# The SSD input tiles count as ready after 17 ticks in place of 12, and the SSD norm's row sums are issued one tick later

## The chip, the cores and the metric

The kernel runs on one core of a Trainium2 chip. The metric is the time of one execution on the device, in microseconds (us). Before the change the median of three runs is 1231.24 us (1230.96 to 1231.58).

A core has engines that run side by side, each through its own list of instructions in order: TensorE (PE: matmuls; its weight loads are shown as PEld), VectorE (DVE), ScalarE (ACT) and GpSimd (POOL); SyncE (SP) issues DMAs. They wait for one another through semaphores. PE writes to PSUM banks, and ACT or DVE must read a bank before PE may use it again.

## The reference, cut to what matters

One layer of a hybrid encoder on 256 tokens, model width 2048, in float32:

1. RMS norm, then one input projection whose columns serve two head groups. The SSD group (Mamba-2) takes x (1024 columns), B and C (256 each), z (1024) and dt (16); the GLA group takes q, k, v, a gate g and a low-rank gate.
2. SSD: x, B and C pass a causal convolution of width 4 over the tokens, then SiLU. With the decays from dt it computes, in chunks, `y = (C B^T, masked and decayed) (x dt) + state term + x d`, multiplies by SiLU(z), and takes an RMS norm over each half of 512 columns.
3. GLA: gated linear attention of 4 heads, its own norm and output gate.
4. Both results together pass the output projection and are added to x. Then a ConvFFN (up projection to 2 x 5632, a convolution of width 3, SiLU gate, down projection), a gate by an embedding of each token, and a final RMS norm.

## The kernel before

**Matmuls.** Everything is kept with channels on partitions and the 256 tokens as columns. Each float32 operand is split in a rounded part (hi) and a rest (lo). A product of one weight tile (128 x 128) with one activation tile is a *pair* of matmuls: L224 multiplies the weights' hi by both parts of the activation (512 columns), L226 the weights' lo by its hi (256 columns, 280 in a chunk's first one). ACT and DVE add the two halves of the bank (`combine`, L236 and L237).

**Weights.** They come from HBM in chunks of 1 MB (16 tiles), four buffers `raw`. `prepare` makes of each half chunk the hi part by a cast on ACT (L191) and the lo part by a subtraction on DVE (L192). There are five buffers of each, so a cast waits until PE has finished the half chunk five halves earlier.

**The input projection** goes through the list `PLAN`, one chunk at a time: v 0 to 3, conv 8 to 11 (B and C), conv 0, v 4, conv 1, v 5, conv 2, v 6, conv 3, v 7, conv 4, q 0, k 0, conv 5, v 8, conv 6, v 9, conv 7, v 10, q 1, k 1, v 11, q 2, k 2, q 3, k 3, then eight chunks z and eight g. A conv, q, k, z or g chunk is 16 pairs into one of four PSUM banks `pm_t`. Four v chunks share two banks, with 24 matmuls a chunk (L911 to L913, 352 columns). Behind each chunk its evacuation is written: for conv `ev_conv` (L561), with the combine, a multiplication by half the norm's factor (L563), the convolution (L565 on ACT, three L568 on DVE) and `half_silu` (a tanh on ACT, L444, then L445 on DVE). Conv 0 to 3 are the x tiles of the SSD's first half (group 0), conv 4 to 7 those of its second.

**Ticks.** All the attention work is written between these matmuls by small tasks (generators). `tick()` counts up after every 4 pairs (4 x 6 matmuls make the 4 ticks of a v chunk) and lets at most one task that is due take its next step. `mark(key, lag)` says that something counts as done `lag` ticks from now; `wait(keys)` holds a task until then. No instruction waits for a tick: they only decide in which place of PE's order, and so roughly when, a step stands. On PE that order is kept as written; the order on ACT and DVE is set by a scheduler that goes by its own estimates of times, so it changes with the places on PE.

**The SSD's tasks.** `ssd_rest` (L701) waits until the four x tiles of a group count as done. Then `ssd_xdt` (L637) transposes them on PE for the first 128 tokens (L640, four instructions into a bank `px_t`) and DVE multiplies by dt (L643) and, for the state, by a decay (L650); two ticks later the same for the other 128 tokens. Five ticks on, `ssd_state` makes the state by one matmul (L657) that ACT copies (L659), and `ssd_out` makes the outputs by 12 matmuls for each half of the group's tiles (L673, two pieces each in the trace), evacuated by DVE (L677). `ssd_front` makes the decays beside it (L615 loads on POOL's queue, L622, L630, L632, L633). After z, `ssd_norm` (L730) waits for the four tiles of a group and calls `norm_task` (L328): the sums over rows, a reciprocal root, two diagonal matrices (L317), and, `lag` ticks later, the matmuls that spread the factor over partitions (L325), its copy (L335) and the scaling and splitting of the four tiles (L737, L271, L272) that the output projection multiplies.

Of the kernel before, what the change touches and what calls it, by code (L numbers as in the profile page):

```python
# [99 lines left out]
def trunk(ctx, tc, wst, wv, xin, pin, prm_d, cst_d, gku_d, out):  # L100
# [14 lines left out]
    def slot(dtype=F32, shape=(128, 512)):  # L115
        return gpool.tile(list(shape), dtype, name="slot")

    def tmp():
        return small.tile([128, T], F32, name="tmp", bufs=10)
# [35 lines left out]
    def mark(key, lag=5):  # L155
        done[key] = now[0] + lag

    def wait(*keys):
        while any(done.get(k, 1 << 30) > now[0] for k in keys):
            yield 0  # L160
# [73 lines left out]
    def combine(ps):  # L234
        t = tmp()
        S.copy(out=t, in_=ps[:, T:2 * T])  # L236
        V.tensor_tensor(out=t, in0=ps[:, 0:T], in1=t, op=ALU.add)  # L237
        return t
# [20 lines left out]
    def pcol(i):  # L259
        return prm[:, i:i + 1]  # L260
# [8 lines left out]
    def split(src):  # L269
        a = slot(F32R, (128, 2, T))  # L270
        S.copy(out=a[:, 0, :], in_=src)  # L271
        V.tensor_tensor(out=a[:, 1, :], in0=src, in1=a[:, 0, :].bitcast(F32), op=ALU.subtract)  # L272
        return a
# [54 lines left out]
    def norm_task(sq, width, then, lag=6):  # L328
        with tc.high_priority(offset=2 * PRIO):
            r = sq.token(width)  # L330
            d = sq.spread(r)
        yield lag
        ps = sq.rows(d)
        keep = small.tile([128, T], F32, name="rb", bufs=2)
        S.copy(out=keep, in_=ps)  # L335
        then(r, keep)
# [105 lines left out]
    def half_silu(c, out):  # L442
        t = tmp()
        S.activation(out=t, in_=c, func=AF.Tanh)  # L444
        V.scalar_tensor_tensor(out=out, in0=t, scalar=1.0, in1=c, op0=ALU.add, op1=ALU.mult)  # L445
# [115 lines left out]
    def ev_conv(i, ps):  # L561
        v = combine(ps)
        V.tensor_tensor(out=v, in0=v, in1=state["rh"], op=ALU.mult)  # L563
        c = tmp()
        S.activation(out=c, in_=v, func=AF.Identity, scale=pcol(P_CW + 36 + i),  # L565
                     bias=cbh[:, i:i + 1])
        for s in (1, 2, 3):
            V.scalar_tensor_tensor(out=c[:, s:], in0=v[:, :T - s],  # L568
                                   scalar=pcol(P_CW + 12 * (3 - s) + i), in1=c[:, s:],
                                   op0=ALU.mult, op1=ALU.add)  # L570
        if i < 8:
            if i % 2 == 0:
                state["xs"] = slot()
            ssd_x[i] = state["xs"][:, (i % 2) * T:(i % 2 + 1) * T]
            half_silu(c, ssd_x[i])
        elif i < 10:
            half_silu(c, bT[:, (i - 8) * T:(i - 7) * T])
        else:
            half_silu(c, cT[:, (i - 10) * T:(i - 9) * T])
        mark(("conv", i), 12)  # L580

    cb = {}
    mt = {}
# [131 lines left out]
    ssd_sq = {}  # L715
# [14 lines left out]
    def ssd_norm():  # L730
        for g in range(2):
            yield from wait(("z", 4 * g + 3))

            def then(r, keep):
                for i in range(4 * g, 4 * g + 4):
                    y = ssd_y[i]
                    V.scalar_tensor_tensor(out=y, in0=y, scalar=pcol(P_SN + i), in1=keep,  # L737
                                           op0=ALU.mult, op1=ALU.mult)
                    mix[i] = split(y)
            yield from norm_task(ssd_sq[g], 512, then, 13)  # L740


    gq = [slot(), slot()]
# [121 lines left out]
    def ev_in(kind, i, ps):  # L865
        if kind == "conv":
            ev_conv(i, ps)
        elif kind == "q":
            ev_qk(gq, i, ps, 128.0 ** -0.5)
        elif kind == "k":  # L870
            ev_qk(gk, i, ps, 1.0)
            mark(("k", i))
        elif kind == "z":
            ev_z(i, ps)
        else:
            ev_g(i, ps)

    vps = None
    for ci, (kind, i) in enumerate(PLAN):
# [13 lines left out]
        if ci == 4:  # L893
            start(after(1, norm_task(sq_mix, 2048, in_norm, 6)))
            start(ssd_front())
            start(ssd_rest())
            start(gla_front())
            start(gla_back())
            start(ssd_norm())
# [64 lines left out]
    conv = {}  # L964
# [226 lines left out]
```

## Time and profile before

| what | value |
|---|---|
| median of three runs | 1231.24 us |
| profiled execution, its own time | 1230.86 us |
| its span, first to last instruction | 1228.9 us |
| mean granted clock of TensorE | 0.996 of full speed |
| PE busy | 1212.1 us, 99% |
| DVE busy | 916.8 us, 75% |
| ACT busy | 685.6 us, 56% |

The profile is of one execution. Its busy times say how full an engine is over the whole; which stage has the limit is seen in windows and in the timelines, where a row has its start, its length, engine, line and operation, the tile written and those read, and in square brackets the idle time of the engine before it with what ended it. Instructions of one engine overlap a little, so the next start tells better than the length how long one holds its engine. Times are counted from the start of the span.

### The profile page before, as it was taken

The page shows a single profiled execution, that of the slowest core. Times are in us where ns is not written, and L with a number is a line of the kernel's source. Part 1 is how long each engine was busy: PE and PEld are TensorE (multiplying, and loading weights), DVE is VectorE, ACT ScalarE, POOL GpSimd, SP SyncE. Part 2 cuts the span into 40 slices and gives each one's busy share as a digit, 9 for nine tenths or more (in the row PEclk, how much of TensorE's full clock was granted, in tenths as well). Part 3 has the DMA queues.
Part 4 walks back from the last instruction along what each step waited for, and adds up shares of the span by engine and source line. Part 5 has one row for each costly group of instructions (what it writes and reads, how often), then busy time and mean ns, then how long its engine had stood idle before and what let it go on. Part 6 is the DMA issues. An engine that isn't in the chain of part 4 may idle for free.

```text
span 1228.9 us, 18359 instructions
## 1 busy us (share of the span) xinstructions
PE 1212.1 (99%) x7115; PEld 1070.8 (87%) x7115; DVE 916.8 (75%) x1607; ACT 685.6 (56%) x1117; POOL 9.3 (1%) x23
## 2 busy tenths in 40 slices
PE   9998999999999999999999999999999999999996
PEld 8897888888888888888888888888888888888886
DVE  7889776789777788778875555878877876666775
ACT  8675555666544655555553333555555554444664
POOL 0010000000000000000000000000000000000000
PEclk9999999999999999999999999999999999999998
DMA  9855553444555555555555555555555555555632
GB/s 337 307 163 192 182 201 138 171 172 171 183 194 188 190 180 198 188 189 194 183 200 178 203 176 203 176 201 181 197 186 190 192 203 196 181 201 205 218 113 69
DMA packets 37623, 233.20 MB, mean 190 GB/s; under 512 B 4384, under 2 KB 4800, under 8 KB 11936
## 3 DMA queue, kind: packets, MB, share of 16 engines
q1 hardware_dynamic: 36832, 229.92, 53.2%
q0 software_dynamic: 704, 2.11, 0.6%
q8 instruction: 55, 0.90, 0.3%
q14 instruction: 32, 0.26, 0.1%
HBM read 227.81 MB, written 4.21 MB: 189 GB/s over the span
## 4 chain that ended last, share of the span: by engine, by line
PE 93%; DVE 3%; ACT 2%; issue 1%; DMA 1%; SPq 0%; DVEq 0%; ACTq 0%
PE pm_t L224 58%; PE pm_t L226 30%; DVE wlo L192 1%; PE pm_t L912 1%; PE pm_t L911 1%; PE pm_t L913 1%; ACT whi L191 1%; DMA raw<-in_wst_dram 1%; PE px_t L673 0%; ACT xg L264 0%; PE px_t L807 0%; DVE slot L630 0%; PE px_t L789 0%; ACT tmp L285 0%; PE px_t L292 0%
## 5 line engine op out<-in xcount | busy, mean ns | idle before, releaser
L224 PE MATMUL pm_t<-xg,whi 128*128 128x512 f32 x2224 | 778.7, 393 | 0.0
L191 ACT CAST whi<-raw 128x1024 fp32r<-128x1024 f32 (+3 forms) x444 | 445.2, 1007 | 498.8 <-PE pm_t L224 455.7
L192 DVE TENSOR_TENSOR wlo<-raw,whi 128x1024 fp32r<-128x1024 f32 (+3 forms) x444 | 516.9, 1167 | 247.4 <-ACT whi L191 240.8
L226 PE MATMUL pm_t<-xg,wlo 128*128 128x256 f32 (+1 forms) x2224 | 623.8, 280 | 0.0
L224 PEld LDWEIGHTS pm_t<-xg,whi 128*128 128x128 f32 x2224 | 417.1, 188 | 91.9 <-issue 0.5
L226 PEld LDWEIGHTS pm_t<-xg,wlo 128*128 128x128 f32 x2224 | 420.9, 189 | 0.0
L224 PE MATMUL pm_t<-slot,whi 128*128 128x512 f32 x960 | 333.2, 391 | 0.0
L226 PE MATMUL pm_t<-slot,wlo 128*128 128x256 f32 (+1 forms) x960 | 269.0, 280 | 0.0
L224 PEld LDWEIGHTS pm_t<-slot,whi 128*128 128x128 f32 x960 | 179.5, 187 | 39.4
L226 PEld LDWEIGHTS pm_t<-slot,wlo 128*128 128x128 f32 x960 | 181.4, 189 | 0.0
L977 DVE SCALAR_TENSOR_TENSOR tmp<-tmp,prm 128x255 f32<-128x255 f32 (+1 forms) x176 | 84.5, 480 | 4.5 <-ACT tmp L974 1.5
L237 DVE TENSOR_TENSOR tmp<-pm_t,tmp 128x256 f32<-128x256 f32 x139 | 58.0, 418 | 1.0 <-ACT tmp L236 0.9
L932 DVE TENSOR_TENSOR x<-x,pm_t 128x256 f32<-128x256 f32 x96 | 40.0, 419 | 23.5 <-PE pm_t L226 22.2
L974 ACT ACTIVATE tmp<-tmp,prm 128x256 f32<-128x256 f32 x88 | 52.3, 595 | 0.8 <-DVE tmp L972 0.8
L236 ACT COPY tmp<-pm_t 128x256 f32<-128x256 f32 x139 | 49.8, 358 | 1.2 <-PE pm_t L226 1.2
L972 DVE TENSOR_TENSOR tmp<-tmp,rb 128x256 f32<-128x256 f32 x88 | 37.1, 421 | 1.4
L912 PE MATMUL pm_t<-wlo,xg 128*128 128x352 f32 x96 | 31.2, 325 | 0.8 <-DVE wlo L192 0.6
L911 PE MATMUL pm_t<-whi,xg 128*128 128x352 f32 x96 | 31.7, 330 | 0.3 <-ACT whi L191 0.3
L913 PE MATMUL pm_t<-whi,xg 128*128 128x352 f32 x96 | 30.9, 322 | 0.0
L286 DVE TENSOR_TENSOR acc<-acc,tmp 128x256 f32<-128x256 f32 x69 | 28.9, 418 | 2.6 <-ACT tmp L285 2.6
L285 ACT ACTIVATE tmp<-x 128x256 f32<-128x256 f32 x59 | 23.1, 407 | 4.7 <-DVE x L1025 4.7
L264 ACT ACTIVATE xg<-x,prm 128x256 fp32r<-128x256 f32 x48 | 23.1, 506 | 0.0
(204 smaller groups left out, 578.8 us busy)
## 6 DMA issues: line engine op xcount, KB each, us to landing
raw<-in_wst_dram SPq DMA_DIRECT2D x200, 1024.0 KB, 4.9
raw<-in_wv_dram SPq DMA_DIRECT2D x8, 704.0 KB, 4.3
raw<-in_wv_dram SPq DMA_DIRECT2D x8, 352.0 KB, 9.0
x<-in_xin_dram SPq DMA_DIRECT2D x4, 512.0 KB, 8.7
pp<-slot SPq DMA_DIRECT2D x8, 256.0 KB, 9.1
slot<-csd POOLq DMA_DIRECT2D x8, 256.0 KB, 4.1
slot<-pp SPq DMA_DIRECT2D x8, 256.0 KB, 5.4
out_dram<-raw SPq DMA_DIRECT2D x8, 256.0 KB, 3.6
```

The lines of the kernel that those rows point to most:

```text
L191: S.copy(out=hi[:, sl], in_=raw[:, rs])
L192: V.tensor_tensor(out=lo[:, sl], in0=raw[:, rs], in1=hi[:, sl].bitcast(F32), op=ALU.subtract)
L224: PE.matmul(ps, lhsT=hi, rhs=both, start=first, stop=False)
L226: PE.matmul(ps[:, 0:w], lhsT=lo, rhs=both[:, 0:w], start=False, stop=last)
L236: S.copy(out=t, in_=ps[:, T:2 * T])
L237: V.tensor_tensor(out=t, in0=ps[:, 0:T], in1=t, op=ALU.add)
L911: PE.matmul(o, lhsT=xa[k][:, 0, tk], rhs=hi[:, w], start=k == 0, stop=False)
L912: PE.matmul(o, lhsT=xa[k][:, 0, tk], rhs=lo[:, w], start=False, stop=False)
L913: PE.matmul(o, lhsT=xa[k][:, 1, tk], rhs=hi[:, w], start=False, stop=k == KT - 1)
L932: V.tensor_tensor(out=x[:, i, :], in0=x[:, i, :], in1=ps[:, h * T:(h + 1) * T], op=ALU.add)
L974: S.activation(out=c, in_=v, func=AF.Identity, scale=pcol(P_FW + 176 + ch), bias=pcol(P_FB + ch))
L977: V.scalar_tensor_tensor(out=c[:, s:], in0=v[:, :T - s], scalar=pcol(P_FW + 88 * (2 - s) + ch), in1=c[:, s:], op0=ALU.mult, op1=ALU.add)
```

## The change

The mark behind a conv tile's evacuation gets a lag of 17 ticks in place of 12 for the x tiles (0 to 7); B and C keep 12. The SSD norm's `norm_task` gets a lag of 14 ticks in place of 13.

```diff
@@ -577,7 +577,7 @@
             half_silu(c, cT[:, (i - 10) * T:(i - 9) * T])
-        mark(("conv", i), 12)
+        mark(("conv", i), 12 if i >= 8 else 17)
@@ -737,7 +737,7 @@
                     mix[i] = split(y)
-            yield from norm_task(ssd_sq[g], 512, then, 13)
+            yield from norm_task(ssd_sq[g], 512, then, 14)
```

No instruction is added or taken away; they stand in other places. PE, at the first group's transposes: before, they stand between the chunks q 0 (`pm_t_1386`) and k 0 (`pm_t_1442`). `slot_936` holds conv 0 and 1, `slot_1157` conv 2 and 3.

```order
L224 MATMUL pm_t_1386<-xg_355,whi_1317 128x512
L226 MATMUL pm_t_1386<-xg_355,wlo_1318 128x256
L640 MATMUL px_t_1419<-cst_85,slot_936 128x128 x2
L640 MATMUL px_t_1419<-cst_85,slot_1157 128x128 x2
L224 MATMUL pm_t_1442<-xg_270,whi_1378 128x512
L226 MATMUL pm_t_1442<-xg_270,wlo_1379 128x280
```

Now, on PE, they stand in conv 5 (`pm_t_1480`), behind k 0 (here `pm_t_1433`):

```order
L224 MATMUL pm_t_1433<-xg_355,whi_1382 128x512
L226 MATMUL pm_t_1433<-xg_355,wlo_1383 128x256
L224 MATMUL pm_t_1480<-xg_270,whi_1425 128x512
L226 MATMUL pm_t_1480<-xg_270,wlo_1426 128x280
L224 MATMUL pm_t_1480<-xg_273,whi_1425 128x512
L226 MATMUL pm_t_1480<-xg_273,wlo_1426 128x256
L224 MATMUL pm_t_1480<-xg_276,whi_1425 128x512
L226 MATMUL pm_t_1480<-xg_276,wlo_1426 128x256
L224 MATMUL pm_t_1480<-xg_279,whi_1425 128x512
L226 MATMUL pm_t_1480<-xg_279,wlo_1426 128x256
L640 MATMUL px_t_1489<-cst_85,slot_936 128x128 x2
L640 MATMUL px_t_1489<-cst_85,slot_1157 128x128 x2
```

They moved back by the 16 pairs of k 0 and four pairs of conv 5. The second four, the state's L657 and the first L673 move by as many ticks; those of the second group too.

DVE, from conv 3's last instruction (L445 to `slot_1157`) on, before. `tmp_1363` is conv 4, `tmp_1428` q 0, `wlo_1493` the second half of v 8.

```order
L445 SCALAR_TENSOR_TENSOR slot_1157<-tmp_1266,tmp_1261 128x256
L237 TENSOR_TENSOR tmp_1363<-pm_t_1321,tmp_1363 128x256
L563 TENSOR_TENSOR tmp_1363<-tmp_1363,rh_686 128x256
L568 SCALAR_TENSOR_TENSOR tmp_1367<-tmp_1363,prm_83,tmp_1367 128x255
L568 SCALAR_TENSOR_TENSOR tmp_1367<-tmp_1363,prm_83,tmp_1367 128x254
L568 SCALAR_TENSOR_TENSOR tmp_1367<-tmp_1363,prm_83,tmp_1367 128x253
L445 SCALAR_TENSOR_TENSOR slot_1372<-tmp_1373,tmp_1367 128x256
L643 TENSOR_TENSOR slot_1424<-px_t_1419,dta_393 128x512
L237 TENSOR_TENSOR tmp_1428<-pm_t_1386,tmp_1428 128x256
L650 TENSOR_TENSOR slot_1426<-slot_1424,esuf_397 128x512
L749 SCALAR_TENSOR_TENSOR slot_404<-tmp_1428,rb_682 128x256
L643 TENSOR_TENSOR slot_1464<-px_t_1459,dta_393 128x512
```

Now, on DVE, from the last convolution steps of conv 4 on. `wlo_1544` and `wlo_1548` are the two halves of conv 6, `tmp_1419` is q 0, `tmp_1466` k 0, `wlo_1617` a half of v 9, `tmp_1529` conv 5.

```order
L192 TENSOR_TENSOR wlo_1544<-raw_1541,whi_1543 128x1024
L568 SCALAR_TENSOR_TENSOR tmp_1367<-tmp_1363,prm_83,tmp_1367 128x253
L192 TENSOR_TENSOR wlo_1548<-raw_1541,whi_1547 128x1024
L445 SCALAR_TENSOR_TENSOR slot_1372<-tmp_1373,tmp_1367 128x256
L237 TENSOR_TENSOR tmp_1419<-pm_t_1386,tmp_1419 128x256
L237 TENSOR_TENSOR tmp_1466<-pm_t_1433,tmp_1466 128x256
L749 SCALAR_TENSOR_TENSOR slot_404<-tmp_1419,rb_682 128x256
L749 SCALAR_TENSOR_TENSOR slot_406<-tmp_1466,rb_682 128x256
L643 TENSOR_TENSOR slot_1494<-px_t_1489,dta_393 128x512
L192 TENSOR_TENSOR wlo_1617<-raw_1614,whi_1616 128x704
L237 TENSOR_TENSOR tmp_1529<-pm_t_1480,tmp_1529 128x256
L650 TENSOR_TENSOR slot_1496<-slot_1494,esuf_397 128x512
```

Both halves of conv 6 now stand ahead of conv 4's L445 and q 0's combine, and all of these ahead of L643 and L650. Up to conv 4's combine (`tmp_1363`) the kinds of DVE's instructions stand as before.

ACT, at the copy of the first group's state (L659), before: behind casts of v 8 (`whi_1492`) and conv 6 and a copy of k 0.

```order
L191 CAST whi_1492<-raw_1486 128x704
L191 CAST whi_1562<-raw_1560 128x1024
L236 COPY tmp_1482<-pm_t_1442 128x256
L191 CAST whi_1566<-raw_1560 128x1024
L659 COPY slot_1523<-px_t_1521 128x512
```

Now, on ACT, behind casts of v 9 and conv 7 (`whi_1687`) and the convolution's first step of conv 5:

```order
L191 CAST whi_1620<-raw_1614 128x704
L768 ACTIVATE slot_1562<-slot_983,be_1559 128x64
L191 CAST whi_1687<-raw_1685 128x1024
L565 ACTIVATE tmp_1533<-tmp_1529,cbh_387,prm_83 128x256
L659 COPY slot_1597<-px_t_1595 128x512
```

The cast just ahead is now that of a later chunk, and L565 stands between it and the copy.

## Rows read from the trace of the kernel before

**Rows 1.** The page: busy time, share of the span, instructions of each engine.

```profile
PE 1212.1 (99%) x7115; PEld 1070.8 (87%) x7115; DVE 916.8 (75%) x1607; ACT 685.6 (56%) x1117; POOL 9.3 (1%) x23
```

**Rows 2.** PE's waits, whole run: releaser, us in total, times, longest.

```profile
PE px_t L640 <- DVE slot L445: 4.0, 1, 4.0
```

**Rows 3.** PE's timeline around the first group's transposes.

```profile
105.23 0.39 PE L224 MATMUL pm_t<-xg,whi 128*128 128x512 f32 x1
...
110.80 0.49 PE L640 MATMUL px_t<-cst,slot 128*128 128x128 f32 x3
115.25 0.33 PE L640 MATMUL px_t<-cst,slot 128*128 128x128 f32 x1 [3.96 <-DVE slot L445]
115.33 0.48 PE L224 MATMUL pm_t<-xg,whi 128*128 128x512 f32 x1
...
119.77 0.60 PE L640 MATMUL px_t<-cst,slot 128*128 128x128 f32 x4
120.12 0.47 PE L224 MATMUL pm_t<-xg,whi 128*128 128x512 f32 x1
```

**Rows 4.** DVE's timeline, conv 3's evacuation and what follows.

```profile
102.15 0.42 DVE L237 TENSOR_TENSOR tmp<-pm_t,tmp 128x256 f32<-128x256 f32 x1
...
114.78 0.41 DVE L445 SCALAR_TENSOR_TENSOR slot<-tmp 128x256 f32<-128x256 f32 x1
115.11 0.42 DVE L237 TENSOR_TENSOR tmp<-pm_t,tmp 128x256 f32<-128x256 f32 x1
...
119.06 0.68 DVE L643 TENSOR_TENSOR slot<-px_t,dta 128x512 f32<-128x512 f32 x1
119.66 0.41 DVE L237 TENSOR_TENSOR tmp<-pm_t,tmp 128x256 f32<-128x256 f32 x1
120.00 0.68 DVE L650 TENSOR_TENSOR slot<-slot,esuf 128x512 f32<-128x512 f32 x1
...
124.14 1.23 DVE L192 TENSOR_TENSOR wlo<-raw,whi 128x1024 fp32r<-128x1024 f32 x1 [1.73 <-ACT whi L191]
```

**Rows 5.** Windows: busy us (instructions) of each engine, granted clock, DMA share, GB/s.

```profile
90.00:110.80 20.80, 20.80 (x124) 18.80 (x123) 20.77 (x38) 14.68 (x23) 0.54 (x1) 1.00 0.71 245
110.80:115.33 4.53, 0.57 (x6) 0.34 (x5) 4.53 (x11) 2.09 (x4) 0.00 (x0) 1.00 0.28 66
115.33:119.77 4.44, 4.44 (x18) 3.83 (x19) 3.12 (x8) 1.28 (x3) 0.00 (x0) 0.62 0.41 173
119.77:137.00 17.23, 17.14 (x129) 14.52 (x128) 13.15 (x32) 8.03 (x15) 1.61 (x3) 1.00 0.45 149
```

**Rows 6.** PE's timeline: the second group's L325, the output projection's first pair.

```profile
294.04 0.39 PE L325 MATMUL px_t<-diag,ones_r 128*128 128x256 f32 x1 [0.21 <-ACT diag L317]
...
302.60 0.39 PE L224 MATMUL pm_t<-slot,whi 128*128 128x512 f32 x1
```

**Rows 7.** DVE's timeline: the split of the second group's four tiles.

```profile
299.83 1.42 DVE L272 TENSOR_TENSOR slot<-slot 128x256 fp32r<-128x256 f32 x4
```

**Rows 8.** ACT's timeline: casts, a conv bias, the state's copy.

```profile
116.02 0.60 ACT L565 ACTIVATE tmp<-tmp,cbh,prm 128x256 f32<-128x256 f32 x1 [1.86 <-DVE tmp L563]
...
119.85 0.78 ACT L191 CAST whi<-raw 128x704 fp32r<-128x704 f32 x1 [0.90 <-PE pm_t L224]
...
123.06 1.05 ACT L191 CAST whi<-raw 128x1024 fp32r<-128x1024 f32 x1 [2.44 <-PE pm_t L224]
...
128.26 0.58 ACT L659 COPY slot<-px_t 128x512 f32<-128x512 f32 x1 [1.33 <-PE px_t L657]
```

**Rows 9.** PE's timeline: the state, the outputs, a v chunk.

```profile
127.21 1.02 PE L657 MATMUL px_t<-slot 128*128 128x512 f32 x2
128.16 1.84 PE L673 MATMUL px_t<-slot 128*64 128x128 f32 x24
...
131.42 0.32 PE L911 MATMUL pm_t<-whi,xg 128*128 128x352 f32 x1
...
131.90 0.32 PE L911 MATMUL pm_t<-whi,xg 128*128 128x352 f32 x1
...
132.47 1.53 PE L673 MATMUL px_t<-slot 128*64 128x128 f32 x24
```

## The prediction

> **What bounds the kernel now.** I read the page's busy shares first: PE 1212.1 of 1228.9 us [rows 1], so nearly every microsecond that PE loses or gets back moves the end. Next come PE's own waits. The longest is a single one of 4.0 us, at the transposes of line 640 [rows 2]. PE's timeline shows its place: three of the transposes' pieces start at 110.80, the last one at 115.25, and the next weights' matmul at 115.33 [rows 3]. DVE tells why. Conv 3's combine (L237) starts at 102.15, and its last instruction (L445), for which the transposes wait, at 114.78 [rows 4]; between 90 and 110.8 DVE is busy 20.77 of 20.80 us, and during the wait 4.53 of 4.53 [rows 5]. So PE came to a transposition whose input a full DVE had not finished. The wait has a second price: the granted clock of 115.33 to 119.77 is 0.62, most of it at the lower level of 1.2 GHz, against 1.00 (2.4 GHz) before and after [rows 5].
>
> **What the edits remove.** At full clock the 16 pairs (L224 and L226) of chunk q0 go from 105.23 to 110.80 [rows 3]: 5.57 us, 0.348 each. Four transposes undisturbed take 119.77 to 120.12, 0.35 [rows 3].
> - The wait: 110.80 to 115.33 is 4.53; less the 0.35 that the transposes cost anyway: 4.18 us.
> - The clock: 115.33 to 119.77 holds 8 pairs in 4.44, of which 8 x 0.348 = 2.79 are due: 1.65 us.
>
> Together 5.83 us, if the input is ready in the new place. Five ticks are four for the chunk k0 and one in conv 5, 20 pairs; the order of PE shows just this. Without a wait k0 starts at 110.80, conv 5 at 116.37, its transposes at 110.80 + 20 x 0.348 = 117.76. DVE's order up to conv 3's L445 and conv 4's combine behind it is the same in both kernels, and DVE was full up to there, so L445 still ends at 114.78 + 0.41 = 115.19 [rows 4]. Margin 2.5 us. The second set of four follows 8 pairs later and has its input then.
>
> The norm's row sums one tick (4 pairs, 1.39 us) later: in the second group L325 waits 0.21 for its diagonal matrix [rows 6], and 1.39 more covers that: 0.21 gained. What stands behind them: the scaled and split tiles (L737, L272), done at 299.83 + 1.42 = 301.25 [rows 7], while the output projection takes the first of them in its fifth pair, 302.60 + 4 x 0.348 = 303.99 [rows 6]. Of these 2.74 the tick takes 1.39 and 1.35 are left: hidden. The first group comes chunks earlier and has more. The conv tiles 8 to 11 keep their 12 ticks.
>
> **What they add.** PE no longer rests, so what it needs between 116 and 135 it needs up to 5.8 us earlier. I follow the orders of ACT and DVE after the change.
> - Conv 6's second half: its cast needs the buffer that conv 5's first half frees, at 116.37 + 8 x 0.348 + 0.35 = 119.50. ACT starts such a cast 0.08 after the release (119.77 and 119.85), and from the cast's start to the end of the subtraction it is 123.06 to 124.14 + 1.23, 2.31 [rows 3, 4, 8]: 121.89. In DVE's new order conv 4's L445 and q0's combine stand right behind it (0.33 to the next start, and 0.42 long [rows 4]): 122.64. PE needs this combine, which frees q0's PSUM bank, when it opens the second bank of chunk v8: conv 5 ends at 119.50 + 2.79 + 0.35 = 122.64, and three matmuls (131.42 to 131.90 [rows 9]) later it is 123.12. Margin 0.48.
> - The state matmul (L657) comes after v8's 24 matmuls of 0.16: 126.48. DVE has until then k0's combine and two L749 (0.34 each, less than their 0.42 since neighbours overlap, as 114.78 + 0.41 and 115.11 show), L643 0.60, a subtraction of 704 columns (704/1024 of 1.23: 0.85, an estimate), a combine 0.34, L650 0.68 [rows 4]: 122.64 + 3.49 = 126.13. Margin 0.35.
> - The copy of the state (L659), for which the first set of L673 matmuls waits after a third of its pieces. In ACT's new order a cast of 1024 columns, freed only by v8's last matmul, and a conv bias (L565) stand ahead of it: 126.48 + 0.08 + 1.05 + 0.60 + 0.58 [rows 8] = 128.79 at most. PE has meanwhile done L657 (127.21 to 128.16, 0.95) and a third of its 24 pieces (0.51): 127.94. It waits 0.85 at most. Before it lost 0.31 there: the first 24 pieces took 1.84, the second, which wait for nothing, 1.53 [rows 9]. Added: 0.54 at most, 0.4 with the overlaps.
>
> The margins of 0.35 and 0.48 are as large as the error of such sums. A new wait on them costs at least nothing, at most what the old one did, 4.18 + 1.65. I take 0.2 for both together, by the nearest row, the 0.31 that PE loses at L673 at the end of a similarly short chain. The second group has the same copy; 0.1 for it. POOL's loads for the second half's decays (L615) wait for L657 and L673 and move with them, but the decays that read them stand well behind in DVE's order; nothing. SP's order of DMAs is unchanged.
>
> **Sum.** 5.83 + 0.21 - 0.4 - 0.2 - 0.1 = 5.34, taken as 5.3. The profiled execution took 1230.86 (span 1228.9): 1225.56. The median 1231.24 is 0.38 higher: 1225.9.
>
> A page speaks against such thin margins. "TensorE: Matmul & The Clock Gate" of the Trainium skill (section "A second HAM failure mode: psum-queue depth-cycling") says that frequent small pauses between groups of matmuls can make the clock swing between its two levels. The trace does not show it so far: 119.77 to 137 holds the pause at L673 and dozens of short matmuls, and its granted clock is 1.00 [rows 5]. By the rule the new pauses would bring the last of the rivals below.
>
> **Rivals.**
> - *A thin margin breaks.* The chain of conv 6's cast, its subtraction and q0's combine gets one more pair of cast and subtraction ahead of it (2.31). PE waits 2.31 - 0.48 = 1.83 at v8: 1227.7; if the clock falls again, 1.65 more: 1229.4. For it: two margins on one chain, and DVE has 4.53 + 3.12 + 13.15 = 20.80 us of work between 110.80 and 137 [rows 5], for which PE leaves only 26.20 - 5.83 = 20.37. Against it: part of that work (L630 of the second half) moves behind conv 6 in the new order.
> - *It doesn't dissolve.* L445 is still late at 117.76. It would need 2.5 us more on a DVE queue that is the same up to there. The wait would then stand at conv 5 with its clock; time about 1231.
> - *The clock swings.* The small new waits between 116 and 137 take PE to the lower level for the whole stretch. The price by rows: 4.44 for 2.79, 59% more. Over 17.23 us [rows 5] that is 10.2, so 1225.9 + 10.2 = 1236. It ends over 0.2% slower than before from 7.8 us of loss on (5.3 + 2.46), that is from 13.2 us at such a clock. Against it: the waits of 0.31 and 0.21 left the clock alone.
>
> **How the numbers follow.** 0.2% is 2.46 us, about the least that a measurement of this kernel can tell from no change. Forecast 0.75, its own range 1224.8 (none of the new waits: 6.04 off, less the scatter of the runs, 0.3) to 1227.2. The broken margin 0.13, at 1227.7 to 1229.4, of which 0.01 lies within 0.2%. Not dissolved 0.05 and small mixtures 0.03, both no change. The swinging clock 0.04. Faster 0.87, same 0.09, slower 0.04. The range 1224.8 to 1229.4 leaves about 0.12 out.
>
> **What would show it.** Right: no wait at L640, granted clock 1.00 between 110 and 120, a wait of some 0.7 us at L673 for L659, and L325's second wait gone. The step on the margins is wrong if PE waits at v8's L911 for L237 or at L657 for L650. The forecast is wrong if L640 still waits for L445, or if a stretch after 116 has a clock well under 1.

## The result, and the profile after

The changed kernel takes 1225.58 us (median of five runs, 1225.06 to 1226.08), the kernel before in the same comparison 1231.58 (five runs, 1230.96 to 1232.07): a ratio of 0.995, 95% interval 0.9936 to 0.9963, some 6 us less. A later comparison of the same two gave 0.9949 (0.9937 to 0.9962). The profiled executions are 5.8 apart, 1225.06 after against 1230.86 before, with spans of 1223.1 and 1228.9. The forecast was 1225.9.

The page's busy shares of after, to be laid beside [rows 1]:

```profile
PE 1210.1 (99%) x7115; PEld 1068.5 (87%) x7115; DVE 915.9 (75%) x1607; ACT 685.2 (56%) x1117; POOL 9.5 (1%) x23
```

The same instructions, and PE is busy 2.0 us less, most of it in the matmuls that ran at the lower clock before. The rest of the gain was idle time. PE's waits of after (releaser, us in total, times, longest), against [rows 2]:

```profile
PE px_t L352 <- DVE slot L349: 1.3, 1, 1.3
PE px_t L673 <- ACT slot L659: 1.0, 2, 0.7
...
PE px_t L325 <- ACT diag L317: 0.5, 1, 0.5
```

L640 is gone from the list, L673 is new (before, 0.2 us of idle time in brackets stand at it, or 0.67 lost by starts, as reckoned further down). The first row is an early wait that both kernels have. PE's timeline of after, against [rows 3, 9]:

```profile
110.73 0.39 PE L224 MATMUL pm_t<-xg,whi 128*128 128x512 f32 x1
...
117.69 0.60 PE L640 MATMUL px_t<-cst,slot 128*128 128x128 f32 x4
118.04 0.48 PE L224 MATMUL pm_t<-xg,whi 128*128 128x512 f32 x1
...
120.95 0.60 PE L640 MATMUL px_t<-cst,slot 128*128 128x128 f32 x4
...
122.79 0.33 PE L911 MATMUL pm_t<-whi,xg 128*128 128x352 f32 x1
...
123.28 0.32 PE L911 MATMUL pm_t<-whi,xg 128*128 128x352 f32 x1
...
126.64 1.02 PE L657 MATMUL px_t<-slot 128*128 128x512 f32 x2
127.59 0.66 PE L673 MATMUL px_t<-slot 128*64 128x128 f32 x8
128.91 1.09 PE L673 MATMUL px_t<-slot 128*64 128x128 f32 x16 [0.66 <-ACT slot L659]
```

The first row is the start of k0, 0.07 us earlier than in the profile of before (110.80), ahead of anything that moved. The transposes start at 117.69 (worked out: 117.76), all four without a pause, and v8's second bank opens at 123.28. DVE's timeline of after, against [rows 4], tells how much time was left:

```profile
114.71 0.43 DVE L445 SCALAR_TENSOR_TENSOR slot<-tmp 128x256 f32<-128x256 f32 x1
...
120.70 1.22 DVE L192 TENSOR_TENSOR wlo<-raw,whi 128x1024 fp32r<-128x1024 f32 x1 [0.87 <-ACT whi L191]
121.84 0.42 DVE L445 SCALAR_TENSOR_TENSOR slot<-tmp 128x256 f32<-128x256 f32 x1
122.18 0.75 DVE L237 TENSOR_TENSOR tmp<-pm_t,tmp 128x256 f32<-128x256 f32 x2
...
125.25 0.68 DVE L650 TENSOR_TENSOR slot<-slot,esuf 128x512 f32<-128x512 f32 x1
```

Conv 3's L445 ends at 115.14, 2.5 us ahead of its need. The combine of q0 is the first of the two L237 at 122.18, done by 122.60, 0.68 ahead of 123.28. L650 ends at 125.93, 0.71 ahead of the state matmul. ACT's timeline of after, against [rows 8], shows the copy of the state:

```profile
126.84 1.04 ACT L191 CAST whi<-raw 128x1024 fp32r<-128x1024 f32 x1 [0.89 <-PE pm_t L913]
127.79 0.60 ACT L565 ACTIVATE tmp<-tmp,cbh,prm 128x256 f32<-128x256 f32 x1
128.29 0.56 ACT L659 COPY slot<-px_t 128x512 f32<-128x512 f32 x1
```

It ends at 128.85 behind the cast and L565; PE's third of the pieces was through at 128.25, and it waits. Windows of after (columns as in [rows 5]; there the second and third of its stretches had the clock 1.00 and 0.62):

```profile
110.80:120.00 9.20, 9.20 (x56) 8.15 (x55) 8.33 (x17) 4.71 (x8) 0.00 (x0) 1.00 0.56 194
120.00:131.00 11.00, 10.34 (x75) 8.71 (x74) 10.30 (x24) 6.61 (x15) 1.42 (x3) 1.00 0.40 119
```

PE is full to 120 at 2.4 GHz; the 0.66 missing from the second stretch is the wait at L673. The second group's L325 [rows 6] is now one row:

```profile
290.08 0.40 PE L325 MATMUL px_t<-diag,ones_r 128*128 128x256 f32 x2
290.32 0.39 PE L224 MATMUL pm_t<-xg,whi 128*128 128x512 f32 x1
```

**A part that the prediction doesn't have** is at the end. Where the last transpositions (L1065) start, after is 5.13 us ahead, but its span is 5.8 shorter. DVE's timeline before, in the final norm:

```profile
1218.13 0.16 DVE L1089 SCALAR_TENSOR_TENSOR rt<-rr 128x2 f32<-128x2 f32 x1 [0.27 <-ACT rr L1088]
1218.44 0.69 DVE L1079 COPY slot<-px_t 128x512 f32<-128x512 f32 x1
1219.04 0.15 DVE L1090 TENSOR_TENSOR rt<-rt,rv 128x2 f32<-128x2 f32 x1
1219.23 0.16 DVE L1091 SCALAR_TENSOR_TENSOR rr<-rt,rr 128x2 f32<-128x2 f32 x1
1219.42 1.41 DVE L1100 TENSOR_SCALAR raw<-px_t,rr 128x512 f32<-128x512 f32 x2
```

and after:

```profile
1213.01 0.16 DVE L1089 SCALAR_TENSOR_TENSOR rt<-rr 128x2 f32<-128x2 f32 x1 [0.27 <-ACT rr L1088]
1213.20 0.16 DVE L1090 TENSOR_TENSOR rt<-rt,rv 128x2 f32<-128x2 f32 x1
1213.40 0.16 DVE L1091 SCALAR_TENSOR_TENSOR rr<-rt,rr 128x2 f32<-128x2 f32 x1
1213.48 0.68 DVE L1079 COPY slot<-px_t 128x512 f32<-128x512 f32 x1
1214.08 1.40 DVE L1100 TENSOR_SCALAR raw<-px_t,rr 128x512 f32<-128x512 f32 x2
```

Before, a copy of 512 columns (L1079) stands inside the chain that yields the norm's factor, and every scaling (L1100, and ACT's) waits for it; after, it stands behind the chain. From the start of the last piece of L1065 to the end it is 9.90 before and 9.23 after: 0.67 (spans are rounded to 0.1, so each such figure is good to 0.05). The change touches nothing there; the scheduler ordered two DVE instructions the other way.

### The profile page after: what moved, and what is told of

It is laid out like the page before. It is cut to its first block, busy times and chain, and to the rows that moved or that the text cites. A ratio compares the mean times of both kernels' runs of the same rounds, so it can differ in the third digit from the quotient of the medians.

```text
span 1223.1 us, 18362 instructions
## 1 busy us (share of the span) xinstructions
PE 1210.1 (99%) x7115; PEld 1068.5 (87%) x7115; DVE 915.9 (75%) x1607; ACT 685.2 (56%) x1117; POOL 9.5 (1%) x23
## 4 chain that ended last, share of the span: by engine, by line
PE 96%; ACT 2%; DVE 1%; DMA 1%; SPq 0%; issue 0%; DVEq 0%
PE pm_t L224 60%; PE pm_t L226 31%; PE pm_t L912 1%; PE pm_t L913 1%; PE pm_t L911 1%; DMA raw<-in_wst_dram 1%; ACT whi L191 1%; PE px_t L673 0%; ACT xg L264 0%; PE px_t L807 0%; PE px_t L789 0%; ACT tmp L285 0%; PE px_t L292 0%; SPq L171 0%; PE px_t L325 0%
## 5 line engine op out<-in xcount | busy, mean ns | idle before, releaser
L237 DVE TENSOR_TENSOR tmp<-pm_t,tmp 128x256 f32<-128x256 f32 x139 | 57.9, 418 | 1.0 <-ACT tmp L236 0.9
```

## The experiments

Theory: the gain is L640's wait and its clock, less a new wait at L673, plus two parts of the norm edit (L325 and the order at the end). Rivals: that the shifted places of everything else made it (then taking the wait away elsewhere would not give it), and that the norm edit carries a good part.

**One edit at a time.** `conv17_only` has the first edit alone:

```diff
-        mark(("conv", i), 12)
+        mark(("conv", i), 12 if i >= 8 else 17)
```

> The first edit alone (17 ticks for the x tiles, the norm's lag stays 13). Theory: the wait of 4 us at L640 and its low clock go, and nothing else; the offset of PE against the kernel before at the chunk z/g boundary was 4.85 us in the changed kernel, so 4.8 us faster, about 1226.7. The last matmul-to-end stretch stays as before (9.9 us), since DVE's order at the end is that of before. Rival (the shorter end of the changed kernel came from its granted clock or from scatter, not from an order): the end is as likely short here as long, 1226.1 to 1226.7.

Measured: 1225.94 (1225.81 to 1228.67), ratio 0.9959 (0.9946 to 0.9972), no wait at L640, clock 1.00. Its waits:

```profile
PE px_t L673 <- ACT slot L659: 1.0, 2, 0.7
...
PE px_t L325 <- ACT diag L317: 0.7, 2, 0.4
```

L673 is as in after, both waits at L325 as before. At its last transposition it is 4.93 us ahead of before (0.18 of it from the start of k0 on, ahead of anything that moved), and the end takes 9.93 from there: the long end. The median is 0.8 below the 1226.7 expected. `norm14_only` has the second edit alone:

```diff
-            yield from norm_task(ssd_sq[g], 512, then, 13)
+            yield from norm_task(ssd_sq[g], 512, then, 14)
```

> The second edit alone (the norm's lag 14, 12 ticks stay). Theory: two small gains. The second group's L325 no longer waits (0.2 to 0.5 us), and at the end of the program the copy L1079 (0.68 us) stands behind L1091 in DVE's order, no longer between L1089 and L1090, which takes 0.6 us from the path to the last outputs. Together 0.8 to 1.1 us faster, about 1230.5; the wait of 4 us at L640 and a clock near 0.6 after it remain. Rival (the second edit does only what it says): 0.2 us faster at most, about 1231.4.

Measured: 1230.18 (1229.66 to 1233.14), ratio 0.9993 (0.9984 to 1.0002): too small for the runs to tell from nothing. Its trace has the wait of 4.0 at L640, one wait at L325 less (0.5 us gained there against before), and an end of 9.24, the short one. So the first edit makes nearly all of the gain. L325 belongs to the second. The short end came with the second edit here and in after, but that edit alone does not decide it: lag13, lag14 and lag15 below have it too, and their copy L1079 stands between L1089 and L1090 as before, with ends of 9.9. Why the scheduler orders the pair as it does stays open. That the second edit and the end are worth some 1 us (0.30 left of L325's 0.47, as reckoned further down, and 0.67) is read from traces alone; by the runs conv17_only and after are not told apart.

**The order at the end alone.** `tail_only` is the kernel before with the copy held behind L1091:

```diff
-        (S.copy if c == 0 else V.tensor_copy)(out=early[c], in_=banks[0, c])
+        if c == 0: S.copy(out=early[c], in_=banks[0, c])
...
+        tc.keep_in_program_order(V.tensor_copy(out=early[1], in_=banks[0, 1]))
```

> The kernel before with one thing changed: at the end DVE's copy L1079 is put behind the last step of the root (L1091) by an order kept as written. Theory: 0.6 us faster, about 1230.9, with the end after the last matmul 0.6 us shorter; the wait at L640 stays at 4 us. Rival (the end differs by clock or scatter): no change, 1231.5.

Measured: 1230.87 (1230.5 to 1232.44), ratio 0.9995 (0.9986 to 1.0004), which the runs can't tell from nothing, and 9.10 from the last transposition to the end against 9.90. By its own span it gained nothing (1228.9), because in this execution the wait at L640 cost more clock; its windows, against [rows 5]:

```profile
110.80:115.33 4.53, 0.56 (x6) 0.33 (x3) 4.53 (x11) 2.01 (x4) 0.00 (x0) 0.82 0.31 75
115.33:119.77 4.44, 4.44 (x15) 3.77 (x15) 3.12 (x8) 1.28 (x3) 0.00 (x0) 0.50 0.39 162
```

The wait is the same 4.0 us (3.97 here, 3.96 before), but the clock is down before it ends and stays so through the whole second stretch. The 8 pairs take 115.23 to 120.52, 5.29 us, of which 2.79 are due: 2.50 lost, where the profile of before lost 1.65.

**The wait taken away without moving anything on PE.** `ready_tile` is the kernel before, but the first group's transposes read tiles that have long been written; so its first SSD group is computed from other data:

```diff
-                         ssd_x[g * 4 + j][:, c * 128:(c + 1) * 128], ident)
+                         (bT[:, j * 128:(j + 1) * 128] if g == 0 else ssd_x[g * 4 + j][:, c * 128:(c + 1) * 128]), ident)
```

> The kernel before with its transposes in their old place, but those of the first group read the tile of B, which is ready long before, in place of the x tiles: the SSD's result of the first group is that of other data. It takes away what L640 waits for and moves nothing on PE. Theory (the loss is the wait and the clock behind it, not the place): 4.0 us of wait and about 1.65 of clock go; some come back, since L643 and L650 then stand in a DVE queue that is still full with conv 3 (up to 1.5 us at L657 or L673). 4 to 5.6 us faster, 1226 to 1227.5, granted clock 1.00 throughout 110 to 130. Rival (the later place itself gains, for example by freeing DVE): under 2 us faster, and PE waits for other work of DVE instead, with the clock down again.

Measured: 1226.65 (1225.98 to 1227.31), ratio 0.996 (0.9946 to 0.9974). PE's timeline:

```profile
110.52 0.60 PE L640 MATMUL px_t<-cst,slot 128*128 128x128 f32 x4
...
121.97 1.12 PE L657 MATMUL px_t<-slot 128*128 128x512 f32 x2 [0.62 <-DVE slot L650]
123.03 0.44 PE L673 MATMUL px_t<-slot 128*64 128x128 f32 x4
124.05 1.31 PE L673 MATMUL px_t<-slot 128*64 128x128 f32 x20 [0.58 <-DVE slot L643]
```

The transposes stand where they stood before and don't wait, and the clock is 1.00. The gain is there without the new places, which rules out the first rival. But two waits on DVE of 0.6 have come: with the transposes left at their early place, what follows them is asked of the full DVE too early. At the last transposition it is 4.61 ahead, against conv17_only's 4.93; 0.28 and 0.18 of these stood there before the transposes.

**How many ticks.** `lag13`, `lag14` and `lag15` are after with 13, 14 and 15 in place of 17 (the norm at 14 in all):

```diff
-        mark(("conv", i), 12 if i >= 8 else 17)
+        mark(("conv", i), 12 if i >= 8 else 13)
```

> 13 ticks for the x tiles (the norm's lag 14): the transposes come 4 pairs into k0, at 112.2 us, 3 us before their input. Theory: a wait of 2.6 us remains. Whether a wait of this length still costs the clock is open: if it does, as after the 4 us wait (1.65 to 3 us lost in the profiles so far), the kernel is about 1.9 us faster than before, 1229.7; if it doesn't, 3.5 to 4.5 us, 1227.2 to 1228. The end is long (L1079 before L1090). Rival (the place gains, not the wait): as fast as with 17.

> 14 ticks for the x tiles (the norm's lag 14): the transposes come 8 pairs into k0, at 113.6. Theory: a wait of 1.2 us, and no lower clock behind it, since waits of 0.3 to 1.3 us left the clock at 1.00 so far: about 4.7 us faster than before, 1226.9; with the clock's price as well, 1229.

> 15 ticks for the x tiles (the norm's lag 14): the transposes come 12 pairs into k0, at 115.0, within 0.3 us of the end of conv 3's L445. Theory: no wait over 0.2 us, clock 1.00, and the wait at L673 for the state's copy is 0.3 us as before since L659 is not behind L565: main stream as fast as with 17 or 0.4 us faster; the end is 0.67 us longer (L1079 before L1090): 1225.5 to 1226.3. Rival (the five ticks are needed): a wait of over 1 us at L640 or behind it.

Measured: 1228.39 (0.997, 0.9959 to 0.9982), 1226.84 (0.9957, 0.9944 to 0.9969) and 1225.56 (0.9945, 0.9933 to 0.9958). The first lies between the two times expected, 1229.7 with the clock's price and 1227.2 to 1228 without; its profiled execution took 1229.37 and was the slowest of the six. PE's timeline of lag13 and then of lag14:

```profile
111.75 0.49 PE L640 MATMUL px_t<-cst,slot 128*128 128x128 f32 x3
114.80 0.33 PE L640 MATMUL px_t<-cst,slot 128*128 128x128 f32 x1 [2.56 <-DVE slot L445]
```

```profile
113.92 0.49 PE L640 MATMUL px_t<-cst,slot 128*128 128x128 f32 x3
115.60 0.33 PE L640 MATMUL px_t<-cst,slot 128*128 128x128 f32 x1 [1.18 <-DVE slot L445]
```

Each tick takes some 1.4 us off the wait, the time of its 4 pairs. Their windows in one stretch, lag13 first:

```profile
115.33:119.77 4.44, 4.44 (x21) 3.86 (x20) 2.52 (x6) 1.89 (x4) 0.00 (x0) 0.62 0.36 143
```

```profile
115.33:119.77 4.44, 4.17 (x26) 3.72 (x27) 3.15 (x8) 1.70 (x3) 0.00 (x0) 1.00 0.89 339
```

In these profiles, one execution each, the wait of 2.56 us still took the clock down (its 8 pairs lost 1.63), the one of 1.18 did not (0.12 lost, which 8 pairs behind transposes lose in after without a wait too). Up to then the longest wait within the stream that left the clock alone was the 0.66 of after; the 1.3 in the expectation of lag14 can only be L352's, ahead of the program's first matmul. At 15 the wait at L640 is gone, and none at L673 is listed either:

```profile
126.48 1.84 PE L673 MATMUL px_t<-slot 128*64 128x128 f32 x24
```

This is the row of before [rows 9], 0.31 over the undisturbed 1.53, since there L659 stands ahead of L565 on ACT. So three ticks are enough here, but barely: conv 3's L445 ends at 115.62 in this profile (115.20 + 0.42, a row not shown), while the transposes start at 115.66; in lag15_tail below it ends at 116.22 and they start at 115.99, and only the fourth reads its tile. The two more ticks of the change buy the 2.5 us of margin and bring the wait at L673.

**A version faster than both.** `best1` is after with the outputs (L673) one tick behind the state (L657), so that the copy L659 has time, and with the order at the end held as in tail_only:

```diff
-            ssd_state(g)
+            ssd_state(g); yield 1
```

> The changed kernel with one tick more between the state's matmul (L657) and the outputs (L673), in both groups, and DVE's order at the end kept as written (L1079 behind L1091). Theory: the two waits at L673 for L659 (0.66 and 0.33 us) go, the end stays short: 1.0 us faster than the changed kernel, 1224.5, and no PE wait over 0.2 us between 60 us and the end. Rival (the next margin breaks, for example L677 on DVE holds the weights' subtraction): no gain, 1225.5.

Measured: 1224.24 (1222.87 to 1225.31), ratio to before 0.9934 (0.992 to 0.9948). PE's timeline:

```profile
128.46 1.02 PE L657 MATMUL px_t<-slot 128*128 128x512 f32 x2
...
130.81 1.53 PE L673 MATMUL px_t<-slot 128*64 128x128 f32 x24
```

The 24 pieces take 1.53, no wait at all. A last comparison ran it again, beside after and beside 15 ticks with the order at the end held (no further tick):

> The changed kernel, unchanged, on the same chip as the two that follow, so that medians can be compared: 1225.6, with the waits of 0.66 and 0.33 us at L673 and the short end (9.2 us after the last matmul's start).

> 15 ticks with the end's order kept as written (L1079 behind L1091). Theory: the gains are separate terms and add: the waits at L673 that 17 ticks brought are gone by the place of L659 on ACT, and the end is short. 0.6 to 0.8 us faster than the changed kernel, about 1224.9. Rival (the order of the end is not what made it short): 1225.5, as the 15 ticks alone.

> 17 ticks, one tick between state and outputs, the end's order kept: again about 1.0 us faster than the changed kernel on the same chip, 1224.5; within 0.3 us of the 15 ticks with the short end, since both have no wait on PE between 60 and 290 us. Rival (its first median was low by the scatter of the start): as the changed kernel.

| | median (range of 5 runs), us | ratio to before (95%) |
|---|---|---|
| before (9 runs) | 1231.51 (1230.66 to 1233.65) | |
| after_again | 1225.76 (1225.22 to 1226.31) | 0.9949 (0.9937 to 0.9962) |
| lag15_tail | 1224.7 (1224.21 to 1226.12) | 0.9943 (0.9931 to 0.9956) |
| best1_again | 1224.66 (1223.93 to 1225.13) | 0.994 (0.9926 to 0.9954) |

In this comparison best1 is 1.1 us faster than after, and the two sets of five runs don't overlap. lag15_tail has the same median; its runs overlap with after's, so its own gain over after is likely and not shown.

## Why the prediction was right

The mechanism, the place and the time held: the wait and its clock are gone, and ready_tile shows that taking the wait away gives the gain. That the time came out so near is in part luck, since the terms that were off nearly cancel. The steps, in us, between the two profiled executions:

| step | predicted | shown |
|---|---|---|
| wait at L640 | 4.18 | 4.18, gone |
| its clock | 1.65 | 1.53 in the profiled execution; 2.4 in two others |
| copy L659, both groups | -0.4 - 0.1 | -0.75 |
| thin margins | -0.2 | 0 |
| L325 | 0.21 | 0.47 |
| elsewhere in the stream | not priced | -0.4 |
| start of the profiled execution | not priced | 0.07 |
| order at the end | not seen | 0.67 |
| sum | 5.3 | 5.8 |

- *The clock.* The 1.65 counted all that the 8 pairs took over 2.79. But in after 8 pairs behind four transposes that don't wait take 118.04 to 120.95, 2.91. So 0.12 of the 1.65 is no price of the clock: 1.53. The term is also one execution's, the one that the forecast starts from; tail_only and norm14_only paid 0.85 more.
- *L659.* The order on ACT and its end were right (at most 128.79; 128.85 measured). Before, the first sets of the two groups take 1.84 [rows 9] and 1.89: 0.31 and 0.36 over 1.53. After, the first goes from 127.59 to 128.91 + 1.09 = 130.00, 2.41, so 0.88 over. The second group's rows, first before and then after, where they give 0.54:

```profile
176.71 1.89 PE L673 MATMUL px_t<-slot 128*64 128x128 f32 x24
```

```profile
179.87 0.66 PE L673 MATMUL px_t<-slot 128*64 128x128 f32 x8
180.85 1.09 PE L673 MATMUL px_t<-slot 128*64 128x128 f32 x16 [0.33 <-ACT slot L659]
```

  Together 1.42 less 0.67, 0.75. What was mis-sized is the 0.54 at most that the first group should add, shaved to 0.4 for overlaps that did not come (0.57 measured, a little over the most), and the second group's 0.1, which was 0.18.
- *Margins.* 0.48 and 0.35 by the sums, 0.68 and 0.71 measured: PE came 0.16 later than reckoned to both (123.28 for 123.12, 126.64 for 126.48), and L650 0.20 sooner. No wait, so the 0.2 kept for them was not needed.
- *L325.* The 0.21 in brackets is the idle time between the modelled end of one matmul and the start of the next. By starts, the two matmuls held PE before from 293.55 to 294.26, 0.71, and after from 290.08 to 290.32, 0.24: 0.47. The wait at L640 had been priced by starts, this one not. The rows of before, around the L325 of [rows 6]:

```profile
293.55 0.28 PE L325 MATMUL px_t<-diag,ones_r 128*128 128x256 f32 x1
...
294.26 0.40 PE L224 MATMUL pm_t<-xg,whi 128*128 128x512 f32 x1
```

- *Elsewhere.* By the starts of chunks, less what each profile was ahead at k0, the first edit is worth 4.75 in after and in conv17_only: 4.18 + 1.53 - 0.75 - 0.21. After L325 after is 5.32 ahead, and 5.13 at the last transposition. These 0.19 go with the second edit: norm14_only and lag13 lose them in the same chunks, conv17_only does not, so that of L325's 0.47 some 0.30 are left. The two losses, 0.4 in all, were not traced to single instructions.
- *The end.* The prediction followed the new order only from 110 to 137 and at L325. The order at the end was to be seen in the order of DVE's instructions before any run. That it fell the good way at 17 ticks and not at 13 to 15 is luck.

The losses at L659 and elsewhere and the gains at L325 and the end nearly cancel, so the sum was nearer than its terms. No margin broke, the wait dissolved, and the clock stayed at 1.00 through the new waits. The page on the clock gate in the Trainium skill ("TensorE: Matmul & The Clock Gate", "A second HAM failure mode: psum-queue depth-cycling") describes a swing under frequent small pauses, and neither after (waits of 0.66 and 0.33) nor lag14 (1.18) has one.

## What to carry to other kernels

A wait of the full engine is priced by starts, not by the bracket: the next start less the start of the waiting group, less what the group takes undisturbed, and then the pairs behind it at the lower clock, against as many pairs behind an undisturbed group. The cure needs just the ticks that cover the wait (here 3 of 1.4 us for 4.18, with almost no margin left); beyond the ticks that a margin needs a consumer only moves towards other work on the engines that feed it, and the copies and combines there are to be followed in the new order. Where a scheduler decides, the order is to be compared to the very end of the program, since a shift by a tick or two can flip a pair of instructions, and flip it back, over nine hundred microseconds on, and what has to stay is better held by an order written out.

## What the runs showed of the hardware

- The price in clock of one wait is not one number. For the wait of 3.96 to 3.97 us at L640 the 8 pairs behind it lost 1.65 us in the profile of before and 2.50 in that of tail_only, 2.49 in that of norm14_only, where the clock fell at different moments (in before behind the wait, in the other two within it) and came back at different pairs. For 2.56 us they lost 1.63, for 1.18 us 0.12; each of these figures holds the 0.12 that 8 pairs lose behind transposes without any wait. The Trainium skill ("TensorE: Matmul & The Clock Gate", "What's actually happening") says of the clock's rise in a kernel's first microseconds that its moment is not tied to the kernel's start and so varies from run to run; that the moment of the fall varies too is what the three profiles show. It fits that the runs of before spread over 3.0 us in the last comparison and those of after over 1.1, but the spread has other parts too (profiles differ by over 1 us in when the first v chunk starts, and the runs of conv17_only, whose profile has no such wait, spread over 2.9), so this is not shown.
- A copy of 0.69 us on DVE inside a chain of instructions of 2 columns each cost 0.67 of span: at the program's end nothing covers it.
